# Expert layer of a two-block network: gates scattered into a DRAM table by accumulating indirect DMAs, first product expert by token, second product kept in PSUM

## Chip, core and metric

The kernel runs on one core of one Trainium2 chip. The metric is the device time of one execution in microseconds (us), and less is better.

## What is computed

The program runs two blocks of a network on 256 tokens of width 2048: a gated MLP and a stick-breaking attention, then a convolution and mLSTM mixer, and at the end a product-key expert layer with a layernorm before and after it. Only the expert layer is changed. Its reference, cut:

```python
q = (xt @ wq).reshape(-1, PEER_HEADS, 2, PEER_HALF)
s = jnp.einsum('thpc,hpnc->thpn', q, keys)
sv, si = lax.top_k(s, PEER_TOPK)
cand = (sv[:, :, 0, :, None] + sv[:, :, 1, None, :]).reshape(-1, PEER_HEADS, PEER_TOPK * PEER_TOPK)
cid = (si[:, :, 0, :, None] * N_KEYS + si[:, :, 1, None, :]).reshape(-1, PEER_HEADS, PEER_TOPK * PEER_TOPK)
top_s, top_j = lax.top_k(cand, PEER_TOPK)
eid = jnp.take_along_axis(cid, top_j, axis=-1)
gate = jax.nn.softmax(top_s.astype(jnp.float32), axis=-1)
act = jax.nn.gelu(jnp.einsum('thkd,td->thk', jnp.take(u, eid, axis=0), xt).astype(jnp.float32), approximate=False)
return jnp.einsum('thk,thkd->td', (gate * act).astype(xt.dtype), jnp.take(v, eid, axis=0))
```

There are 16384 experts (128 x 128 keys), 8 heads and 16 experts per head and token. Both kernels compute it densely: the product of all tokens with all of `u`, gelu, times a table of gates that is zero but for the chosen experts, times all of `v`.

## The kernel before

**Weights.** One list, `order`, names every weight tile (128 x 2048 floats, 1 MB) in the order of use. `Stream` loads them ahead on SP's queue (line 105) into 3 buffers `raw`. ScalarE copies each half tile to a float32r part `wh` (line 191, 6 buffers), VectorE makes the rest, `wl` (line 128, 5 buffers). A new tile is loaded when the second `wl` of the tile three before it is made.

**Products.** `gemm` computes a chunk, 256 tokens by 512 outputs, with three matmuls of 512 columns for each block of 128 inputs and each half of the tokens (lines 315 to 317); the activations are the stationary operand. Its result is two PSUM tiles `acc` (two buffers each). Every 12 matmuls (a half tile) it calls `bg.step()`.

**Background work.** `bg` holds generators. Each step advances every one of them by a piece, so their instructions are recorded between the matmuls of the products. No scheduler moves them later: each engine and each DMA queue runs them in this order.

**Expert layer.** Four chunks make the queries (`wq`). For each, `route` finds the top 16 of the product keys for two heads: 26 pieces, in a chain of four routes, the reduces of line 1129 last. Beside them the first product runs: `NU` = 32 units of 512 experts, four weight tiles each; ScalarE applies gelu and SP writes the result to the DRAM tensor `Ad` (line 1255). After the last route, `gates_all` transposes indices and gates (line 1166) and makes the table of gates: for each token two matmuls' worth of one-hot rows, built by POOL (lines 1183, 1184) and VectorE (line 1181), a matmul of 256 columns (line 1199), an addition (line 1204), and writes of 512 KB to the DRAM tensor `Gd` (line 1206). `load_v` then loads `Ad` and `Gd` of two units on SP's queue (lines 1215, 1218). `prep_v` multiplies them and transposes the product on PE (line 1236) to get experts on the partitions. The second product runs 16 passes of 4 chunks with `gemm`, and VectorE adds each chunk to the residual `h_res` (line 1287).

```python
    RAW, HI, LO = 3, 6, 5
...
        if j == 1:
            del self.raw[i]
            self._load()
```

Of the kernel before, what the change touches and what calls it, by code (L numbers as in the profile page):

```python
# [7 lines left out]
U32 = mybir.dt.uint32  # L8
# [19 lines left out]
for _n, _w in (("ident", 128), ("le", 128), ("trineg", 128), ("mneg3", 384), ("mbig3", 384),  # L28
               ("iota", 128), ("one", 1), ("negone", 1), ("eps", 1), ("leps", 1)):
    CO[_n] = (sum(w for _, w in CO.values()), _w)  # L30
# [56 lines left out]
class Stream:  # L87
    """Weight tiles in the order of use: loaded ahead, split by halves into two float32r parts."""
# [78 lines left out]
def _block(ctx, tc, A, out):  # L167
# [135 lines left out]
    def gemm(xh, xl, kmap, evac, need={}, by_token=False):  # L303
# [3 lines left out]
        acc = [pp.tile([P, 512], F32, name=nm("acc"), tag=f"acc{t}", bufs=2) for t in range(2)]  # L307
        last = len(kmap) - 1

        def mm(t, kk, wh, wl, k, first, fin):  # L310
# [4 lines left out]
            E.matmul(acc[t], a, wa, start=first, stop=False)  # L315
            E.matmul(acc[t], a, wb, start=False, stop=False)  # L316
            E.matmul(acc[t], b, wa, start=False, stop=fin)  # L317
# [31 lines left out]
        r = evac(acc)  # L349
# [25 lines left out]
    def rstd_of(dst, var, eps):  # L375
        """(var + eps) ** -0.5, a square root and a Newton step."""
# [35 lines left out]
    # ================ layer 0: gated MLP with spatial gating ================  # L412
# [196 lines left out]
    # ================ layer 1: stick-breaking attention ================  # L609
# [47 lines left out]
    def staged(gens, gap=2):  # L657
        """Chains run one stage apart, with `gap` steps of other work between the stages."""
# [75 lines left out]
    def affine_prep(c, d, gname, bname):  # L734
        """h_res*c+d in place, then transposed with gain and bias into two parts."""
# [48 lines left out]
    def residual_affine(gname, bname, alloc):  # L784
        """Gain and bias on the residual itself, in the token layout."""
# [24 lines left out]
    # ================ mLSTM and convolution mixer ================  # L810
# [275 lines left out]
    def route(n, q, before):  # L1086
        """Top 16 of the products of keys for two heads; q: [128 tok, 2, 512]."""
# [8 lines left out]
        for t in range(2):  # L1096
# [13 lines left out]
            for hh in range(2):  # L1110
# [34 lines left out]
    def gates_all():  # L1145
        yield from wait(rts[-1])
        ex = et(0, [16, 16])
        tva = tvs.rearrange("p t h k -> p (t h) k")
        V.tensor_tensor(ex, tva, tva[:, :, 0:1].to_broadcast([P, 16, 16]), op=ALU.subtract)
        act(ex, ex, AF.Exp)  # L1150
        yield
        yield
        es = et(1, [512])[:, 0:16]
        V.tensor_reduce(es, ex, axis=mybir.AxisListType.X, op=ALU.add)
        V.reciprocal(es, es)
        for t in range(2):
            V.tensor_tensor(gat[:, t, 2].rearrange("p (h k) -> p h k", h=8), ex[:, t * 8:(t + 1) * 8],
                            es[:, t * 8:(t + 1) * 8, None].to_broadcast([P, 8, 16]), op=ALU.mult)
        yield
        yield  # L1160
        f5 = ft(5, [4, T])
        i0, i1, gh, gl = (f5[:, j] for j in range(4))
        for s_ in range(3):
            p = ps()
            for t in range(2):
                E.transpose(p[:, t * P:(t + 1) * P], gat[:, t, s_], ident)
            if s_ < 2:
                V.tensor_copy((i0, i1)[s_], p[:, :T])
            else:
                act(gh.bitcast(F32R), p[:, :T], AF.Copy)  # L1170
                V.tensor_tensor(gl, p[:, :T], gh, op=ALU.subtract)
        yield
        yield

        def build(t0):
            """One-hot rows of two tokens: gates (two parts) by first key, ones by second key."""
            a = et(rot("oha", (0, 1, 4)), [2, 2, P], F32R)
            c = et(rot("ohb", (2, 3, 5)), [2, P], F32R)
            for j in range(2):
                t = t0 + j  # L1180
                V.tensor_scalar(a[:, j, 0], C("iota"), i0[:, t:t + 1], gh[:, t:t + 1],  # L1181
                                op0=ALU.is_equal, op1=ALU.mult)
                nc.gpsimd.tensor_scalar(c[:, j], C("iota"), i1[:, t:t + 1], None, op0=ALU.is_equal)  # L1183
                nc.gpsimd.tensor_scalar(a[:, j, 1], C("iota"), i0[:, t:t + 1], gl[:, t:t + 1],  # L1184
                                        op0=ALU.is_equal, op1=ALU.mult)
            return a, c

        ready = [build(0)]
        yield
        ready.append(build(2))  # L1190
        yield
        for b in range(T // 8):
            gsb = ft(rot("gsb", (3, 6)), [8, P])
            for hb in range(4):
                t0 = b * 8 + hb * 2
                a, c = ready.pop(0)
                p = ps().rearrange("p (t s i) -> p t s i", t=2, s=2)
                for j in range(2):
                    E.matmul(p[:, j], c[:, j], a[:, j], start=True, stop=True)  # L1199
                if t0 + 4 < T:  # L1200
                    ready.append(build(t0 + 4))
                d = gsb[:, hb * 2:hb * 2 + 2]
                act(d, p[:, :, 0], AF.Copy)
                V.tensor_tensor(d, p[:, :, 1], d, op=ALU.add)  # L1204
                yield
            nc.sync.dma_start(out=Gd[:, b * 8:(b + 1) * 8, :], in_=gsb)

    gall = bg.add(gates_all())
    vin, wts = {}, {}

    def load_v(u):
        if u >= NU:
            return
        a = ft(4 + u % 2, [2, 512])
        nc.sync.dma_start(out=a, in_=Ad[u])
        g = ft(2 + u % 2, [2, 4, P])
        for t in range(2):
            nc.sync.dma_start(out=g[:, t], in_=Gd[4 * u:4 * u + 4, t * P:(t + 1) * P, :].rearrange("j t i -> t j i"))
        vin[u] = (a, g.rearrange("p t j i -> p t (j i)"))

    def prep_v(pr_):
        w16 = tile("xs", [NKT, T], F32R, bufs=4)
        wts[pr_] = (w16[:, 0:8], w16[:, 8:16])
        for j in range(2):
            a, g = vin.pop(2 * pr_ + j)
            for t in range(2):
                V.tensor_tensor(a[:, t], a[:, t], g[:, t], op=ALU.mult)
            yield
            yield
            put = split_ps(wts[pr_][0], wts[pr_][1], 4 * j)  # L1230
            for pr in range(2):
                p = ps()
                for jj in range(2):
                    for t in range(2):
                        k = pr * 2 + jj
                        E.transpose(p[:, jj * T + t * P:jj * T + (t + 1) * P], a[:, t, k * P:(k + 1) * P], ident)  # L1236
                put(pr, p)
                yield
# [149 lines left out]
```

## Time and profile before

| | |
|---|---|
| median of 3 runs | 3409.7 us (3409.08 to 3410.12) |
| span of the profiled execution | 3406.2 us |
| the median over that span | 3.5 us |
| busy PE, VectorE, ScalarE, POOL | 97%, 61%, 44%, 14% of the span |
| moved by DMA | 668.58 MB, 196 GB/s |

The profiled execution's own time is shown only as its span, from the first to the last instruction. Busy shares are over the whole span; a stage is read from stretches of it. PE counts as busy while a matmul is in the array, with ends that are modelled, so the pace of PE is read from the starts of matmuls and not from its busy share.

### The profile page before, as it was taken

How to read it: one execution, taken by the hardware profiler on the slowest of the kernel's cores; microseconds unless marked ns; L12 is line 12 of the kernel's file. 1: busy time of each engine (PE TensorE's matmuls, PEld its weight loads, DVE VectorE, ACT ScalarE, POOL GpSimd, SP SyncE). 2: the span in 40 equal slices, each digit the busy share in tenths (PEclk: the TensorE clock that was granted, in tenths of full speed). 3: DMA queues.
4: the chain of work that ended last, by engine and by line, in shares of the span. 5: the costliest groups of instructions: out<-in, count | busy, mean ns of one | idle time of the engine just before them, and what ended most of it. 6: DMA issues, size and time to landing. Idle time of an engine off the chain costs nothing.

```text
span 3406.2 us, 39023 instructions
## 1 busy us (share of the span) xinstructions
PE 3317.5 (97%) x14722; PEld 2663.5 (78%) x14722; DVE 2067.0 (61%) x2966; ACT 1507.0 (44%) x1781; POOL 485.7 (14%) x522
## 2 busy tenths in 40 slices
PE   8999999999999999999999999888899999999998
PEld 6888888888888878888878887666678888888886
DVE  6565555565555566555579886555554666666666
ACT  5444444444444544444354444443344444444443
POOL 0000000000000000000000008999970000000001
PEclk9999999999999999999999999999999999999999
DMA  7565555545554445545555656555666666666664
GB/s 260 206 209 175 184 185 179 181 165 180 173 173 161 171 151 201 176 148 198 174 190 206 210 192 218 195 187 197 201 225 235 233 218 222 232 227 233 221 211 148
DMA packets 134348, 668.58 MB, mean 196 GB/s; under 512 B 12177, under 2 KB 45073, under 8 KB 62609
## 3 DMA queue, kind: packets, MB, share of 16 engines
q1 hardware_dynamic: 134160, 666.10, 56.7%
q8 instruction: 116, 1.90, 0.2%
q14 instruction: 72, 0.58, 0.0%
HBM read 630.40 MB, written 35.65 MB: 196 GB/s over the span
## 4 chain that ended last, share of the span: by engine, by line
PE 84%; POOL 14%; DVE 1%; ACT 0%; issue 0%; DMA 0%; SPq 0%; DVEq 0%; POOLq 0%
PE acc L315 27%; PE acc L316 26%; PE acc L317 26%; POOL e L1183 8%; POOL e L1184 6%; PE ms L1236 1%; PE ms L361 1%; PE ms L515 0%; DVE res L1272 0%; PE ms L1099 0%; PE ms L642 0%; PE ms L631 0%; DVE wl L128 0%; PE ms L751 0%; DMA raw<-in_aw_v_dram 0%
## 5 line engine op out<-in xcount | busy, mean ns | idle before, releaser
L128 DVE TENSOR_TENSOR wl<-raw,wh 128x1024 fp32r<-128x1024 f32 x1106 | 1343.9, 1221 | 669.4 <-PE acc L316 552.5
L191 ACT ACTIVATE wh<-raw 128x1024 fp32r<-128x1024 f32 x1106 | 1168.0, 1059 | 1198.5 <-PE acc L317 1136.3
L315 PE MATMUL acc<-wh,xs 128*128 128x512 f32 x4160 | 1662.0, 400 | 13.4 <-ACT wh L191 9.0
L316 PE MATMUL acc<-wl,xs 128*128 128x512 f32 x4160 | 1646.5, 396 | 0.5 <-DVE wl L128 0.5
L317 PE MATMUL acc<-wh,xs 128*128 128x512 f32 x4160 | 1645.9, 396 | 0.0
L315 PEld LDWEIGHTS acc<-wh,xs 128*128 128x128 f32 x4160 | 783.2, 188 | 194.2 <-ACT wh L191 9.0
L317 PEld LDWEIGHTS acc<-wh,xs 128*128 128x128 f32 x4160 | 782.6, 188 | 189.8 <-DVE xs L766 0.4
L316 PEld LDWEIGHTS acc<-wl,xs 128*128 128x128 f32 x4160 | 783.3, 188 | 178.0 <-DVE wl L128 1.0
L1183 POOL TENSOR_SCALAR e<-con,f 128x128 fp32r<-128x128 f32 x256 | 273.7, 1069 | 2053.7 <-ACT f L191 2053.7
L1184 POOL TENSOR_SCALAR e<-con,f 128x128 fp32r<-128x128 f32 x256 | 208.6, 815 | 0.0
L191 ACT ACTIVATE f<-ms 128x256 f32<-128x256 f32 (+3 forms) x153 | 62.7, 418 | 291.5 <-PE ms L1199 264.6
L1204 DVE TENSOR_TENSOR f<-ms,f 128x256 f32<-128x256 f32 x128 | 54.3, 424 | 198.1 <-ACT f L191 198.1
L1275 POOL TENSOR_TENSOR res<-res,xs 128x512 f32<-128x512 f32 x6 | 9.7, 1645 | 861.6 <-DVE res L1272 861.6
L1199 PE MATMUL ms<-e,e 128*128 128x256 f32 x256 | 82.7, 328 | 48.4 <-POOL e L1184 48.4
L1199 PEld LDWEIGHTS ms<-e,e 128*128 128x128 f32 x256 | 47.8, 187 | 92.9 <-POOL e L1184 86.5
L368 DVE TENSOR_TENSOR xs<-ms,xs 128x512 fp32r<-128x512 f32 x76 | 52.0, 690 | 110.1 <-ACT xs L191 110.1
L315 PE MATMUL acc<-wh,f 128*128 128x512 f32 x256 | 102.2, 399 | 0.0
L191 ACT ACTIVATE xs<-ms 128x512 fp32r<-128x512 f32 x76 | 44.8, 597 | 128.9 <-PE ms L1236 121.4
L316 PE MATMUL acc<-wl,f 128*128 128x512 f32 x256 | 101.2, 395 | 0.0
L317 PE MATMUL acc<-wh,f 128*128 128x512 f32 x256 | 101.2, 395 | 0.0
L1287 DVE TENSOR_TENSOR res<-res,acc 128x512 f32<-128x512 f32 x120 | 79.7, 683 | 35.1 <-PE acc L317 35.1
L1181 DVE TENSOR_SCALAR e<-con,f 128x128 fp32r<-128x128 f32 x256 | 83.4, 365 | 0.0
(213 smaller groups left out, 1355.5 us busy)
## 6 DMA issues: line engine op xcount, KB each, us to landing
raw<-in_pu_dram SPq DMA_DIRECT2D x128, 1024.0 KB, 4.9
raw<-in_pv_dram SPq DMA_DIRECT2D x128, 1024.0 KB, 4.8
raw<-in_bwi_dram SPq DMA_DIRECT2D x64, 1024.0 KB, 4.7
raw<-in_w_dram SPq DMA_DIRECT2D x56, 1024.0 KB, 4.7
raw<-in_aw_u_dram SPq DMA_DIRECT2D x32, 1024.0 KB, 4.7
raw<-in_aw_z_dram SPq DMA_DIRECT2D x32, 1024.0 KB, 4.8
raw<-in_awo_dram SPq DMA_DIRECT2D x32, 1024.0 KB, 4.7
raw<-in_aw_v_dram SPq DMA_DIRECT2D x31, 1024.0 KB, 4.8
```

What stands on the lines that cost most here:

```text
L128: self.nc.vector.tensor_tensor(l, raw[:, j * 1024:(j + 1) * 1024], self.hi[q].bitcast(F32), op=ALU.subtract)
L191: S.activation(out, in_, func, **kw)
L315: E.matmul(acc[t], a, wa, start=first, stop=False)
L316: E.matmul(acc[t], a, wb, start=False, stop=False)
L317: E.matmul(acc[t], b, wa, start=False, stop=fin)
L368: V.tensor_tensor(xl[:, k0 + 2 * pr:k0 + 2 * pr + 2, :], p.rearrange("p (k t) -> p k t", k=2), hv.bitcast(F32), op=ALU.subtract)
L1181: V.tensor_scalar(a[:, j, 0], C("iota"), i0[:, t:t + 1], gh[:, t:t + 1], op0=ALU.is_equal, op1=ALU.mult)
L1183: nc.gpsimd.tensor_scalar(c[:, j], C("iota"), i1[:, t:t + 1], None, op0=ALU.is_equal)
L1184: nc.gpsimd.tensor_scalar(a[:, j, 1], C("iota"), i0[:, t:t + 1], gl[:, t:t + 1], op0=ALU.is_equal, op1=ALU.mult)
L1199: E.matmul(p[:, j], c[:, j], a[:, j], start=True, stop=True)
L1204: V.tensor_tensor(d, p[:, :, 1], d, op=ALU.add)
L1287: V.tensor_tensor(d, d, acc[t], op=ALU.add)
```

## The change

`gates_all` goes, and with it all one-hot rows. There are two DRAM tables `Gd`, one for each 128 tokens, expert by token. They are cleared by 32 writes of 512 KB on SP's queue during the output projection of the mixer. `route` also computes the softmax of its two heads and the flat index of each gate, and at its end issues 64 indirect DMAs on POOL: each adds 128 single gates, one of each token, into the table. `gemm_t`, the first product, has the weights as the stationary operand and 256 tokens as columns, so that `Ad` holds experts on the partitions and the transposes of `prep_v` go. The second product keeps its 256 x 2048 sums in all eight PSUM banks over the 16 passes and adds them to `h_res` once.

```diff
+    def gemm_t(xh, xl, evac):
+        acc = [pp.tile([P, 512], F32, name=nm("acc"), tag=f"acc{b}", bufs=2) for b in range(2)]
+        for kp in range(NKT // 2):
+            if kp:
+                bg.step()
+            wh, wl = st.next()
+            for k in range(2):
+                kk = kp * 2 + k
+                for b in range(4):
+                    o = acc[b // 2][:, (b % 2) * T:(b % 2 + 1) * T]
+                    c = k * 512 + b * P
+                    E.matmul(o, wh[:, c:c + P], xh[:, kk], start=kk == 0 and b % 2 == 0, stop=False,
+                             skip_group_check=True)
+                    E.matmul(o, wh[:, c:c + P], xl[:, kk], start=False, stop=False, skip_group_check=True)
+                    E.matmul(o, wl[:, c:c + P], xh[:, kk], start=False, stop=kk == NKT - 1,
+                             skip_group_check=True)
+        evac(acc)
+        bg.step()
...
+    def clear_gates():
+        z = ft(5, [1024])
+        nc.gpsimd.memset(z, 0.0)
+        yield
+        for i in range(16):
+            for t in range(2):
+                nc.sync.dma_start(out=Gd[t][i * 1024:(i + 1) * 1024].rearrange("(p a) c -> p (a c)", p=P), in_=z)
+                yield
+                yield
...
-                    V.tensor_reduce(gat[:, t, s_, head * 16:(head + 1) * 16], oh, axis=mybir.AxisListType.X,
-                                    op=ALU.add)
+                    V.tensor_reduce(key[:, s_], oh, axis=mybir.AxisListType.X, op=ALU.add)
+                V.scalar_tensor_tensor(key[:, 0], key[:, 1], float(P), key[:, 0], op0=ALU.mult, op1=ALU.add)
+                V.tensor_scalar(idx[:, t, head * 16:(head + 1) * 16], key[:, 0], float(P), C("pidx"),
+                                op0=ALU.mult, op1=ALU.add)
                 yield
+            hs = slice(2 * n, 2 * n + 2)
+            ex, es = gat[:, t, hs], ws[:, 192:194]
+            V.tensor_tensor(ex, tvs[:, t, hs], tvs[:, t, hs, 0:1].to_broadcast([P, 2, 16]), op=ALU.subtract)
+            act(ex, ex, AF.Exp)
+            yield
+            V.tensor_reduce(es, ex, axis=mybir.AxisListType.X, op=ALU.add)
+            V.reciprocal(es, es)
+            V.tensor_tensor(ex, ex, es[:, :, None].to_broadcast([P, 2, 16]), op=ALU.mult)
+        for c in range(32):
+            for t in range(2):
+                at = 32 * n + c
+                nc.gpsimd.indirect_dma_start(
+                    out=Gd[t].rearrange("e c -> (e c)")[:, None],
+                    out_offset=bass.IndirectOffsetOnAxis(ap=idx[:, t, at:at + 1], axis=0),
+                    in_=gat[:, t, 2 * n + c // 16, c % 16:c % 16 + 1], in_offset=None, compute_op=ALU.add)
...
-    def gates_all():
...
-            for t in range(2):
-                V.tensor_tensor(a[:, t], a[:, t], g[:, t], op=ALU.mult)
+            V.tensor_tensor(a, a, g, op=ALU.mult)
             yield
             yield
...
+            act(wh[:, 4 * j:4 * j + 4], a, AF.Copy)
+            V.tensor_tensor(wl[:, 4 * j:4 * j + 4], a, wh[:, 4 * j:4 * j + 4].bitcast(F32), op=ALU.subtract)
+            yield
             load_v(2 * pr_ + 2 + j)
 
     def first_v():
-        yield from wait(gall)
+        yield from wait(rts[-1])
+        while not all(u in done_u for u in range(2)):
+            yield
         load_v(0)
         load_v(1)
...
+    ys = [[pp.tile([P, 512], F32, name=nm("y"), tag="ms", bufs=4) for t in range(2)] for n in range(2)]
+    ys += [[pp.tile([P, 512], F32, name=nm("y"), tag=f"acc{t}", bufs=2) for t in range(2)] for n in range(2)]
...
-            gemm(*wts[pr_], [0, 4], ev, {}, pr_ == NP_ - 1 and n == 3)
+            fin = pr_ == NP_ - 1
+            gemm(*wts[pr_], [0, 4], ev if fin else None, {}, fin and n == 3, ys[n], pr_ == 0, fin)
```

The change moves instructions on SP and POOL. SP's queue before, late in the first product, where the first loads of the table stand (`raw` is a weight tile, `Ad` the gelus, `Gd` the table):

```order
L105 DMA raw409_18583<-in_pu_dram 128x2048 [waits DMAHW4_49,DVE_49,Activation_49]
L1255 DMA Ad_11789<-f0_1216_18597 128x1024 [waits Activation_49]
L1206 DMA Gd_11788<-f6_1207_18492 128x1024 [waits DMAHW2_49]
L1215 DMA f4_1217_18602<-Ad_11789 128x1024 [waits DMAHW3_49,PE_49]
L1218 DMA f2_1218_18604<-Gd_11788 128x4x128
L1218 DMA f2_1218_18604<-Gd_11788 128x4x128 [waits DMAHW6_49,DMAHW5_49,DMAHW2_49]
L1215 DMA f5_1219_18607<-Ad_11789 128x1024 [waits Pool_49]
L1218 DMA f3_1220_18609<-Gd_11788 128x4x128 [waits DMAHW7_49]
L1218 DMA f3_1220_18609<-Gd_11788 128x4x128 [waits DMAHW0_49]
L105 DMA raw410_18634<-in_pu_dram 128x2048 [waits DMAHW1_49,DVE_49]
```

SP's queue of the change, where the same loads stand now (`Gd0` and `Gd1` are the two tables, `DMASW` the semaphores of POOL's DMAs):

```order
L105 DMA raw345_15908<-in_pu_dram 128x2048 [waits DMAHW6_49,DVE_49]
L1243 DMA Ad_11167<-f0_747_15934 128x1024 [waits Activation_49]
L1205 DMA f4_748_16005<-Ad_11167 128x1024 [waits DMASW4_49,DMASW3_49,DMASW5_49,DMASW2_49,DMASW6_49,DMASW1_49,DMASW7_49,DMASW0_49,DVE_49]
L1208 DMA f2_749_16007<-Gd0_11165 128x4x128 [waits PE_49]
L1208 DMA f2_749_16007<-Gd1_11166 128x4x128 [waits DMAHW5_49]
L1205 DMA f5_750_16010<-Ad_11167 128x1024
L1208 DMA f3_751_16012<-Gd0_11165 128x4x128 [waits DMAHW7_49]
L1208 DMA f3_751_16012<-Gd1_11166 128x4x128 [waits DMAHW0_49]
L105 DMA raw346_16049<-in_pu_dram 128x2048 [waits DMAHW1_49,DVE_49]
```

Before, they stood behind the gelus of the 27th of 32 units; now they stand behind those of the 11th, in the piece that ends the last route, and the first of them waits for all of POOL's DMAs. The tile of `raw346` is the second of the 13th unit.

POOL's queue before, the first one-hot builds of 512:

```order
L1183 TENSOR_SCALAR e_753_14565<-con_71,f_748_14516 128x128
L1184 TENSOR_SCALAR e_752_14564<-con_71,f_748_14516 128x128
L1183 TENSOR_SCALAR e_755_14589<-con_71,f_748_14516 128x128
L1184 TENSOR_SCALAR e_754_14588<-con_71,f_748_14516 128x128
L1183 TENSOR_SCALAR e_760_14623<-con_71,f_748_14516 128x128
```

POOL's queue of the change, from its first indirect DMA on (256 in all, 64 for each route, the two tables in turn):

```order
L1182 DMA Gd0_11165<-f4_610_11825 2097152x1 [waits DMAHW4_49,DMAHW6_49,DMAHW2_49,DMAHW7_49,DMAHW0_49,DVE_49]
L1182 DMA Gd1_11166<-f4_610_11825 2097152x1 [waits DMAHW5_49,DMAHW3_49,DMAHW7_49,DMAHW1_49,DVE_49]
L1182 DMA Gd0_11165<-f4_610_11825 2097152x1 [waits DMASW0_49]
L1182 DMA Gd1_11166<-f4_610_11825 2097152x1 [waits DMASW1_49]
L1182 DMA Gd0_11165<-f4_610_11825 2097152x1 [waits DMASW2_49]
L1182 DMA Gd1_11166<-f4_610_11825 2097152x1 [waits DMASW3_49]
```

POOL builds nothing now; each of its DMAs but the first two waits until the DMA two before it, the last one into the same table, has landed.

## Rows read from the trace of the kernel before

**Rows 1.** The page: span, busy time by engine, granted clock in 40 slices

```profile
span 3406.2 us, 39023 instructions
PE 3317.5 (97%) x14722; PEld 2663.5 (78%) x14722; DVE 2067.0 (61%) x2966; ACT 1507.0 (44%) x1781; POOL 485.7 (14%) x522
...
PEclk9999999999999999999999999999999999999999
```

**Rows 2.** Windows: stretch, its sum, busy PE PEld DVE ACT POOL, clock, DMA, GB/s

```profile
1710.00:1720.00 10.00, 8.68 (x29) 6.83 (x30) 6.42 (x10) 6.33 (x10) 0.00 (x0) 0.66 0.31 105
...
1800.00:1900.00 100.00, 100.00 (x451) 81.08 (x451) 89.15 (x220) 45.10 (x50) 0.00 (x0) 1.00 0.60 209
...
2200.00:2300.00 100.00, 89.10 (x380) 66.88 (x378) 57.37 (x108) 40.90 (x62) 100.00 (x109) 1.00 0.59 193
...
3000.00:3100.00 100.00, 100.00 (x447) 80.70 (x447) 61.78 (x68) 40.89 (x43) 0.00 (x0) 1.00 0.66 233
```

**Rows 3.** Timeline of PE, one period of the one-hot stage: start us, length

```profile
2299.93 0.28 PE L1199 MATMUL ms<-e,e 128*128 128x256 f32 x1
...
2303.63 0.28 PE L1199 MATMUL ms<-e,e 128*128 128x256 f32 x1
```

**Rows 4.** By source, lines 1199 and 1166 on PE: durations ns, first and last start

```profile
L1199 PE MATMUL ms<-e,e x256: 275/281/388, 2064.7 to 2530.0; 128*128 128x256 f32 x128
...
L1166 PE MATMUL ms<-con,f x6: 271/272/273, 2052.8 to 2053.4; 128*128 128x128 f32 x6
```

**Rows 5.** Timeline of PE in the second product, transposes between matmuls

```profile
2555.44 0.60 PE L1236 MATMUL ms<-con,f 128*128 128x128 f32 x4
...
2558.68 0.60 PE L1236 MATMUL ms<-con,f 128*128 128x128 f32 x4
```

**Rows 6.** Groups by line, PE and PEld: count, busy us, mean ns

```profile
L1236 PE MATMUL ms<-con,f 128*128 128x128 f32 x256 | 38.3, 272 | 0.0
...
L822 PEld LDWEIGHTS ms<-xs,wl 128*128 128x128 f32 x16 | 3.0, 188 | 0.0
```

**Rows 7.** Timeline of PE, the mLSTM gates: 48 matmuls of 256 columns, weights stationary

```profile
1282.65 0.40 PE L316 MATMUL acc<-wl,xs 128*128 128x512 f32 x1
...
1285.22 0.28 PE L821 MATMUL ms<-xs,wh 128*128 128x256 f32 x1
...
1290.87 0.40 PE L315 MATMUL acc<-wh,xs 128*128 128x512 f32 x1
```

**Rows 8.** Timeline of VectorE: the last reduce of the first and the last route

```profile
1819.57 0.42 DVE L1129 TENSOR_REDUCE f<-e 128x16 f32<-128x256 f32 x1
...
2041.07 0.42 DVE L1129 TENSOR_REDUCE f<-e 128x16 f32<-128x256 f32 x1
```

**Rows 9.** Groups by line, POOL

```profile
L1183 POOL TENSOR_SCALAR e<-con,f 128x128 fp32r<-128x128 f32 x256 | 273.7, 1069 | 2053.7 <-ACT f L191 2053.7
L1184 POOL TENSOR_SCALAR e<-con,f 128x128 fp32r<-128x128 f32 x256 | 208.6, 815 | 0.0
```

**Rows 10.** DMA issues: count, KB each, median us from issue to landing

```profile
raw<-in_pu_dram SPq DMA_DIRECT2D x128, 1024.0 KB, 4.9
...
Gd<-f SPq DMA_DIRECT2D x32, 512.0 KB, 6.7
f<-Gd SPq DMA_DIRECT2D x64, 256.0 KB, 6.3
...
out_dram<-res SPq DMA_DIRECT2D x8, 256.0 KB, 2.0
```

**Rows 11.** By source, line 1218 (loads of the table): time to landing

```profile
DMA to landing us min/median/max: 3.0/6.3/8.1
```

**Rows 12.** Waits of SP's queue: us in total, times, longest

```profile
SPq L105 <- DVE wl L128: 2890.1, 535, 13.2
```

**Rows 13.** Groups by line, ScalarE and VectorE

```profile
L191 ACT ACTIVATE wh<-raw 128x1024 fp32r<-128x1024 f32 x1106 | 1168.0, 1059 | 1198.5 <-PE acc L317 1136.3 <-issue 29.0 <-DMA raw<-in_aw_v_dram 12.3
...
L1119 DVE TENSOR_SCALAR f<-f 128x16 uint32<-128x16 uint32 x16 | 2.8, 174 | 0.5
```

More of the change, by code (lines that the diff above doesn't have):

```diff
@@ L28 @@
 for _n, _w in (("ident", 128), ("le", 128), ("trineg", 128), ("mneg3", 384), ("mbig3", 384),
-               ("iota", 128), ("one", 1), ("negone", 1), ("eps", 1), ("leps", 1)):
+               ("iota", 128), ("pidx", 1), ("one", 1), ("negone", 1), ("eps", 1), ("leps", 1)):
     CO[_n] = (sum(w for _, w in CO.values()), _w)
@@ L300, in _block, with gemm @@
     ident = C("ident")
-    def gemm(xh, xl, kmap, evac, need={}, by_token=False):
-        acc = [pp.tile([P, 512], F32, name=nm("acc"), tag=f"acc{t}", bufs=2) for t in range(2)]
+    def gemm(xh, xl, kmap, evac, need={}, by_token=False, acc=None, opens=True, closes=True):
+        if acc is None:
+            acc = [pp.tile([P, 512], F32, name=nm("acc"), tag=f"acc{t}", bufs=2) for t in range(2)]
         last = len(kmap) - 1
@@ L314, in mm @@
             wb = wl[:, k * 512:(k + 1) * 512]
-            E.matmul(acc[t], a, wa, start=first, stop=False)
+            E.matmul(acc[t], a, wa, start=first and opens, stop=False)
             E.matmul(acc[t], a, wb, start=False, stop=False)
-            E.matmul(acc[t], b, wa, start=False, stop=fin)
+            E.matmul(acc[t], b, wa, start=False, stop=fin and closes)
         for i, k0 in enumerate(kmap):
@@ L1042, in _block @@
     bg.finish(*[yt5[k] for k in (("o", 0), ("o", 1), ("cB", 0))])
+    Gd = [dr.tile([NE, P], F32, name=f"Gd{t}") for t in range(2)]
+    Ad = dr.tile([NU, P, 4, T], F32, name="Ad")
+    def clear_gates():
[7 more added lines that the diff above has]
+                yield
+    clear = bg.add(clear_gates())
     for n in range(4):
@@ L1066, in _block @@
     nc.sync.dma_start(out=keysT, in_=A["keysT"])
-    Gd = dr.tile([P, T, P], F32, name="Gd")
-    Ad = dr.tile([NU, P, 2, 512], F32, name="Ad")
     f4 = ft(4, [1024])
-    gat = f4[:, :768].rearrange("p (t s c) -> p t s c", t=2, s=3)
-    tvs = f4[:, 768:].rearrange("p (t h k) -> p t h k", t=2, h=8)
+    idx = f4[:, 0:256].bitcast(U32).rearrange("p (t c) -> p t c", t=2)
+    gat = f4[:, 256:512].rearrange("p (t h k) -> p t h k", t=2, h=8)
+    tvs = f4[:, 512:768].rearrange("p (t h k) -> p t h k", t=2, h=8)
     def topk16(vals, mx, ix):
@@ L1143, in _block @@
         gemm(x3h, x3l, FULL, ev, prep3 if n == 0 else {})
-    def gates_all():
[L1146 to L1155, printed above, removed]
-        for t in range(2):
[L1157 to L1206, printed above, removed]
@@ L1208, in _block @@
-    gall = bg.add(gates_all())
     vin, wts = {}, {}
@@ L1223, in prep_v @@
         wts[pr_] = (w16[:, 0:8], w16[:, 8:16])
+        wh, wl = wts[pr_]
         for j in range(2):
             a, g = vin.pop(2 * pr_ + j)
-            for t in range(2):
-                V.tensor_tensor(a[:, t], a[:, t], g[:, t], op=ALU.mult)
+            V.tensor_tensor(a, a, g, op=ALU.mult)
             yield
             yield
[L1230 to L1238, printed above, removed]
+            act(wh[:, 4 * j:4 * j + 4], a, AF.Copy)
+            V.tensor_tensor(wl[:, 4 * j:4 * j + 4], a, wh[:, 4 * j:4 * j + 4].bitcast(F32), op=ALU.subtract)
+            yield
             load_v(2 * pr_ + 2 + j)
     def first_v():
-        yield from wait(gall)
+        yield from wait(rts[-1])
+        while not all(u in done_u for u in range(2)):
+            yield
         load_v(0)
@@ L1247, in first_v @@
         yield from prep_v(0)
+    done_u = set()
     fv = bg.add(first_v())
@@ L1252, in ev @@
             a = ft(rot("act", (0, 1)), [2, 512])
-            for t in range(2):
-                act(a[:, t], acc[t], AF.Gelu)
-            nc.sync.dma_start(out=Ad[u], in_=a)
-        gemm(x3h, x3l, FULL, ev)
-    bg.finish(gall, fv)
+            for b in range(2):
+                act(a[:, b], acc[b], AF.Gelu)
+            nc.sync.dma_start(out=Ad[u], in_=a.rearrange("p b (e t) -> p (b e) t", e=2))
+            done_u.add(u)
+        gemm_t(x3h, x3l, ev)
+    bg.finish(fv)
     bg.drain()
```

28 lines of the change are left out of this document (13 added, 15 removed).

## The prediction

> **What bounds the kernel now.** I read the page first. PE is busy for 97% of the span, no other engine for more than 61%, and the granted clock is at its upper level, 2.4 GHz, in every slice [rows 1]. So a change is worth what it takes off PE's queue, or adds to it as waits. The windows say where PE does not run full: in 2200 to 2300 us it is at 89 us of 100 while POOL is at 100; in 1800 to 1900 VectorE is at 89, and PE is full all the same [rows 2]. The first is the one-hot stage. Its pace is read from starts: from one pair of one-hot matmuls to the next lie 3.70 us, and in them 12 matmuls of the first product and the pair [rows 3].
>
> **The unit of PE's work.** From 1282.65 to 1285.22 us lie 11 matmuls of 512 columns: 233.6 ns each. From 1285.22 to 1290.87 lie 48 of 256 columns with weights stationary, three to a block, as the new first product has them: 117.7 ns each, or 235.4 for two [rows 7]. Their weight loads last 188 ns and overlap [rows 6].
>
> **Part 1, the one-hot table goes.** 128 pairs run from 2064.7 to 2530.0 us [rows 4], 127 periods in 465.3 us. Their other work is 127 x 12 x 0.2336 = 356.0 us. What is left, and goes, is 109 us. The six transposes of line 1166 end with it, under 1 us.
>
> **Part 2, the transposes of the second product go.** Four transposes and 12 matmuls take 2558.68 - 2555.44 = 3.24 us [rows 5]; less 12 x 0.2336 = 2.80 that is 0.44 us. There are 256 / 4 = 64 such groups [rows 6]: 28 us.
>
> **Part 3, the first product by token.** 32 units x 4 tiles x 24 = 3072 matmuls of 512 columns become 6144 of 256. At 235.4 - 233.6 = 1.8 ns a pair that adds 6 us.
>
> **Part 4, sums kept in PSUM.** 120 additions leave VectorE; PE did not wait for them, so this is worth nothing. The banks of chunks 0 and 1 were idle, those of 2 and 3 are needed two chunks after the last unit's gelu. The first chunk's end in the last pass has the same VectorE work as before.
>
> **Part 5, clearing.** 32 writes of 512 KB replace 32 writes of the same size later [rows 10]. 18 of them stand in a row on SP's queue ahead of the fifth query tile: 9.4 MB. A tile of 1 MB lands in 4.9 us, of which a small transfer takes 2.0 as well, so 2.9 us for each MB [rows 10] and 27 us in all. PE has four query tiles in hand, 4 x 24 x 0.2336 = 22 us, and the pause of the layernorm ahead of them. I take 0; without that cover it costs 15 us at most.
>
> **Part 6, the routes get longer.** Each has 28 pieces for 26. Small VectorE work grows by some 32 x 2 operations of 0.17 us [rows 13] and 8 softmaxes of about 1 us: 20 us over four routes of 75 us, in a stretch where VectorE is at 89% [rows 2]. The five `wl` buffers hide it; I take 0, and 10 us if they don't.
>
> So far: -109 - 1 - 28 + 6 = **-132 us**, if nothing new waits.
>
> **Part 7, the scatter, and who waits for it.** This decides the sign. The first route's last reduce is at 1819.6 us and the fourth's at 2041.1 [rows 8]. With two more pieces of 2.80 us for each route so far, and some 2 us of part 3, the first 64 DMAs are ready at about 1826 us and the last 64 at 2066. Only two of them are in flight at once, because each waits for the one two before. With r the time per DMA, half of one DMA's time from issue to the next start on its table, the last lands at T = the later of 1826 + 256 r and 2066 + 64 r (the two routes between never set it by much).
>
> No row shows a DMA from POOL. The nearest to its issue are POOL's one-hot builds, 1.07 and 0.82 us, mean 0.94 [rows 9]. The nearest to its landing, from below, is the write of 256 KB to DRAM at the program's end, with no weights beside it, 2.0 us [rows 10]; the shortest load of the table amid the weights took 3.0 us [rows 11]; from above the write of 512 KB to the table, 6.7 us [rows 10]. A scatter moves 512 bytes, but beside weights, in a stretch where the DMA engines are 60% busy [rows 2]. I take 2.65 us, between the quiet write and the fastest load: r = (0.94 + 2.65) / 2 = 1.8 us. Ends: 2.0 / 2 = 1.0 us, if the issue lies inside the landing, and (1.07 + 6.7) / 2 = 3.9 us. Nothing excludes either.
>
> Who waits: the first load of `Ad`, on SP's queue, in the piece after the last route. Behind it on the same queue stand five more loads and then every weight tile from the second of the 13th unit on. SP runs its queue in order, and it is kept just ahead of PE: its waits for `wl` buffers are 2890 us in 535 times [rows 12]. PE reaches the 12th unit's start at 2066 us: 2052.8, line 1166, which stood four pieces behind the last route [rows 4], and 4 x 2.80 for the eight more pieces of the routes less those four, and some 2 of part 3. It then holds five tiles, those of that unit and the first of the next, 5 x 48 x 0.1177 = 28 us, and stops at 2094. After T, 2 MB of loads go first (2 x 2.9 us), then the tile lands (4.9, rows 10) and its first half is copied (1.06, rows 13): 12 us. When PE resumes after the pause of the layernorm, the granted clock of the next 10 us is 0.66 [rows 2], so some 7 us are at its lower level, 1.2 GHz, and 3 are lost; the same is put here. So PE loses S = T + 15 - 2094 = T - 2079.
>
> With r = 1.8: T = 1826 + 461 = 2287, S = 208 us. **Sum: -132 + 208 = +76 us**, made on the span of 3406.2 us; the median lies 3.5 us above it, and I carry that over: 3409.7 + 76 = **3486 us**. The sign changes at S = 132, T = 2211, r = 1.50 us, a DMA of 3.0 us.
>
> The Trainium skill, "DMA: Bandwidth & Descriptors", section "Anatomy of one DMA — SWDGE (gpsimd) path", puts a DMA issued from POOL at about 2.0 us fixed plus bytes over 436 GB/s; by it r would be 1.0 and the time 3329 us, against 3486 by the rows; that is the lower end of rival B. No run here shows it yet.
>
> **Rivals.**
> - **B, the scatter is quick enough (faster).** The wait stays, but DMAs take under 3.0 us. For it: the quiet write's 2.0 us, and that each moves 512 bytes. Against: that write had no weights beside it, and has no indices to read. With r = 1.4: T = 2184, S = 105, 3383 us. With r = 1.0, the last route's own 64 set the end: T = 2130, S = 51, 3329 us. It decides at r = 1.50.
> - **C, the scatter is much slower (far slower).** Loads of the table take 6.3 us in the middle [rows 10], and 128 single elements may fare like their 512 short packets. With r = 2.8: T = 2543, S = 464, 3742 us. At r = 3.9 it is 4023 us.
> - **D, the wait hides.** T before 2079 gives the whole -132: 3278 us. Against it: the last 64 DMAs alone need 64 us from 2066 on at r = 1.0.
> - **E, the new first product does not run at the pace of the mLSTM gates.** If each of its 6144 matmuls waited for its whole load of 188 ns, it would add 3072 x (376 - 234) ns = 436 us: about 3920 us with the forecast's wait. Rows 7 speak against it: 48 ran at 117.7 ns.
>
> **How the numbers follow.** The forecast, A, r from 1.53 to 2.4 us (its own range 3416 to 3639): 0.47. C: 0.15. E: 0.01. B: 0.31, of which the lower end, r of 1.2 or less, 0.11. D: 0.01. Within 0.2% (7 us, about what a measurement of this kernel can tell from no change; r from 1.48 to 1.53): 0.05. So faster 0.32, same 0.05, slower 0.63. The range goes from B's lower end, 3329, to C, 3742: below and above it stay about 0.04 and 0.10, and the small bounds of parts 5 and 6 lie inside.
>
> **What would show it.** Right: VectorE, SP and PE idle together from about 2094 us on for some 200 us, the wait of SP named as POOL's scatter; POOL issues 256 DMAs at some 1.8 us each from about 1826 us; no idle PE in the old one-hot stage; matmuls of 256 columns at 118 ns in the first product; the second product without transposes, 28 us shorter. Wrong: if the stop of PE is below 132 us, the kernel is faster and the size of r failed; if there is none, the step that SP's wait starves PE failed; if PE is slower in the first product outside the stop, part 3 failed; if PE waits around 1740 us, part 5 did.

## The result, and the profile after

The kernel after takes 3594.4 us (median of 4 runs, 3592.56 to 3596.41), the kernel before 3409.85 beside it: a ratio of 1.0543 [1.0528, 1.0558], so 185 us slower. The forecast was 76 us slower, 3486. The profiled execution took 3595.13 us, with a span of 3593.3, against the 3406.2 of [rows 1].

The page of the kernel after: span, PE's busy time, and in 40 slices PE's busy tenths and its granted clock:

```profile
span 3593.3 us, 42805 instructions
PE 3239.0 (90%) x17276; PEld 2757.0 (77%) x17276; DVE 1883.8 (52%) x2454; ACT 1481.8 (41%) x1638; POOL 438.1 (12%) x267
...
PE   8999999999999999999999930019999999999998
...
PEclk9999999999999999999999975559999999999999
```

PE was busy for 97% of the span before [rows 1]; now there is one hole, about three and a half slices of 90 us, and the granted clock falls to its lower level (0.5, 1.2 GHz) in it. The windows of the same stretches as in [rows 2], busy PE, PEld, DVE, ACT, POOL, then clock, DMA share and GB/s:

```profile
2000.00:2100.00 100.00, 100.00 (x851) 99.88 (x849) 72.67 (x179) 42.99 (x46) 68.51 (x37) 1.00 0.57 159
2200.00:2300.00 100.00, 0.00 (x0) 0.00 (x0) 0.00 (x0) 0.00 (x0) 83.44 (x55) 0.50 0.22 0
3000.00:3100.00 100.00, 100.00 (x431) 80.12 (x430) 54.91 (x47) 43.74 (x42) 0.00 (x0) 1.00 0.67 237
```

From 2200 to 2300 us only POOL works, and no byte of weights moves. Before, that stretch was the one-hot stage, with PE at 89 us. Of the 851 matmuls from 2000 to 2100 us 843 are the first product's, of 256 columns, and 8 a route's; the starts from 2093.80 to 2099.80 us lie 117.6 ns apart, as in [rows 7]. The group of PE with all the idle time of the hole (left of the bar busy us and mean ns, right of it the idle time and what ended it), the wait of SP's queue (total, times, longest), and SP's timeline around it:

```profile
L368 PE MATMUL acc<-xs,wh 128*128 128x256 f32 x2048 | 573.1, 280 | 310.4 <-ACT wh L191 310.4
```

```profile
SPq L1205 <- DMA Gd<-f: 322.4, 4, 316.9
```

```profile
2074.86 0.33 SPq L1243 DMA_DIRECT2D Ad<-f  x1
2397.83 0.33 SPq L1205 DMA_DIRECT2D f<-Ad  x1
2398.21 0.98 SPq L1208 DMA_DIRECT2D f<-Gd  x2
...
2400.86 1.85 SPq L105 DMA_DIRECT2D raw<-in_pu_dram  x3
```

The first load of `Ad` waits for the last scatter until 2397.8 us, the weights behind it with it, and PE, 310 us idle, waits for a weight tile (`wh`). The place and the chain are the forecast's; the scatter's pace is not. The indirect DMAs by source (duration of the issue, the time that it holds POOL; POOL's idle time that ended with a landing, us and times; the time from the issue's start to the landing), and two windows of them alone (busy POOL with the number issued, clock, DMA share, GB/s):

```profile
L1182 POOL DMA_INDIRECT Gd<-f x256: 1543/1545/2589, 1792.7 to 2394.7; - x128
...
  DMA Gd<-f: 71.3, 43
...
DMA to landing us min/median/max: 2.9/3.0/8.8
```

```profile
1832.00:2080.00 248.00, 162.07 (x87) 1.00 0.69 207
2104.00:2390.00 286.00, 237.18 (x154) 0.50 0.22 0
```

Beside the kernel's other work 87 DMAs take 248 us, **2.85 us each**; in the stop 154 take 286 us, **1.85 us each**. So the pace before the stop, not the one in it, was far from the forecast's 1.8, and the slow part has two candidates. Around 2088 us, where PE is about to run dry, the trace parts them. POOL's timeline:

```profile
2080.51 2.54 POOL L1182 DMA_INDIRECT Gd<-f  x1 [0.31 <-issue]
2083.35 2.51 POOL L1182 DMA_INDIRECT Gd<-f  x1 [0.30 <-issue]
2086.16 2.52 POOL L1182 DMA_INDIRECT Gd<-f  x1 [0.30 <-issue]
2088.99 1.55 POOL L1182 DMA_INDIRECT Gd<-f  x1 [0.30 <-issue]
```

and VectorE's:

```profile
2083.22 1.22 DVE L128 TENSOR_TENSOR wl<-raw,wh 128x1024 fp32r<-128x1024 f32 x1 [1.59 <-PE acc L371]
2086.04 1.23 DVE L128 TENSOR_TENSOR wl<-raw,wh 128x1024 fp32r<-128x1024 f32 x1 [1.60 <-PE acc L371]
```

PE runs until 2100, yet the issue falls from 2.52 to 1.55 us as soon as VectorE's last `wl` is made. So one candidate is VectorE (the issue stretches), the other the weights' traffic (the landing stretches, POOL waits for it).

### The profile page after: what moved, and what is told of

The parts are those of the page before. It is cut to its first block, busy times and chain, and to the rows that moved or that the text cites. A ratio compares the mean times of both kernels' runs of the same rounds, so it can differ in the third digit from the quotient of the medians.

```text
span 3593.3 us, 42805 instructions
## 1 busy us (share of the span) xinstructions
PE 3239.0 (90%) x17276; PEld 2757.0 (77%) x17276; DVE 1883.8 (52%) x2454; ACT 1481.8 (41%) x1638; POOL 438.1 (12%) x267
## 3 DMA queue, kind: packets, MB, share of 16 engines
q8 instruction: 135, 2.21, 0.2%
## 4 chain that ended last, share of the span: by engine, by line
PE 86%; POOL 7%; DMA 2%; issue 2%; DVE 1%; ACT 1%; SPq 0%; DVEq 0%; ACTq 0%
PE acc L317 15%; PE acc L318 15%; PE acc L319 15%; POOL Gd L1182 7%; PE y L317 7%; PE y L319 7%; PE y L318 7%; PE acc L370 6%; PE acc L368 6%; PE acc L371 6%; DMA Gd<-f 2%; PE ms L384 1%; PE ms L538 0%; DMA raw<-in_wq_dram 0%; DVE wl L128 0%
## 5 line engine op out<-in xcount | busy, mean ns | idle before, releaser
L317 PE MATMUL acc<-wh,xs 128*128 128x512 f32 x2112 | 848.2, 402 | 15.5 <-ACT wh L191 9.0
L368 PE MATMUL acc<-xs,wh 128*128 128x256 f32 x2048 | 573.1, 280 | 310.4 <-ACT wh L191 310.4
L318 PE MATMUL acc<-wl,xs 128*128 128x512 f32 x2112 | 838.2, 397 | 0.5 <-DVE wl L128 0.5
L319 PE MATMUL acc<-wh,xs 128*128 128x512 f32 x2112 | 838.1, 397 | 0.0
L368 PEld LDWEIGHTS acc<-xs,wh 128*128 128x128 f32 x2048 | 385.8, 188 | 310.6 <-ACT wh L191 310.6
L370 PE MATMUL acc<-xs,wh 128*128 128x256 f32 x2048 | 574.1, 280 | 0.0
L371 PE MATMUL acc<-xs,wl 128*128 128x256 f32 x2048 | 572.3, 279 | 0.5 <-DVE wl L128 0.5
L317 PEld LDWEIGHTS acc<-wh,xs 128*128 128x128 f32 x2112 | 399.1, 189 | 112.7 <-ACT wh L191 9.0
L1182 POOL DMA_INDIRECT Gd<-f x256 | 427.3, 1669 | 413.1 <-DVE f L1178 273.9
L319 PEld LDWEIGHTS acc<-wh,xs 128*128 128x128 f32 x2112 | 398.7, 189 | 97.1 <-DVE xs L789 0.9
L318 PEld LDWEIGHTS acc<-wl,xs 128*128 128x128 f32 x2112 | 399.3, 189 | 93.8 <-DVE wl L128 1.0
L317 PE MATMUL y<-wh,xs 128*128 128x512 f32 x1024 | 403.5, 394 | 0.0
L319 PE MATMUL y<-wh,xs 128*128 128x512 f32 x1024 | 403.5, 394 | 0.0
L318 PE MATMUL y<-wl,xs 128*128 128x512 f32 x1024 | 403.5, 394 | 0.0
L370 PEld LDWEIGHTS acc<-xs,wh 128*128 128x128 f32 x2048 | 385.3, 188 | 0.0
L1218 DVE TENSOR_TENSOR f<-f,f 128x1024 f32<-128x1024 f32 x32 | 39.0, 1218 | 316.6 <-DMA f<-Gd 316.6
```

The costliest lines, as they stand in the source:

```text
L317: E.matmul(acc[t], a, wa, start=first and opens, stop=False)
L319: E.matmul(acc[t], b, wa, start=False, stop=fin and closes)
L368: E.matmul(o, wh[:, c:c + P], xh[:, kk], start=kk == 0 and b % 2 == 0, stop=False, skip_group_check=True)
L370: E.matmul(o, wh[:, c:c + P], xl[:, kk], start=False, stop=False, skip_group_check=True)
L371: E.matmul(o, wl[:, c:c + P], xh[:, kk], start=False, stop=kk == NKT - 1, skip_group_check=True)
L1182: nc.gpsimd.indirect_dma_start(out=Gd[t].rearrange("e c -> (e c)")[:, None], out_offset=bass.IndirectOffsetOnAxis(ap=idx[:, t, at:at + 1], ...
```

## The experiments

The theory: parts 1 to 6 gave what the sum says, and the loss is SP's in-order wait for the scatter; the scatter is slow beside weights and VectorE work. Rivals: the new products themselves are slower, or the scatter hurts in another way than by the stop.

### Taking the wait away, or the scatter

**e3_none**: `for c in range(32)` at the scatter becomes `range(0)`; all gates are left out and the table stays zero.

> The changed kernel without any indirect DMA (all gates are left out; the tables are zero). Theory: no stop of PE in the first product, and the time is that of the other parts of the change alone, 3410 - 132 + 5 = 3283 us. Rival (part of the loss lies in other parts, such as the longer routes or the product by token): above 3300 us.

3281.3 us, 0.9619 [0.9603, 0.9635]. The group that sat idle for 310 us:

```profile
L368 PE MATMUL acc<-xs,wh 128*128 128x256 f32 x2048 | 572.2, 279 | 0.0
```

The second product takes 716 us for its 3072 matmuls, 2546.6 to 3262.7: 233 ns each, with nothing between them. Without the scatter the change saves 126 us of span and 130 of the median, so the whole loss comes with the scatter. That it is the wait, and not the DMAs as such, is for the next run to show.

**e1_late**: the loads are recorded behind the 30th unit of the first product.

```diff
-        while not all(u in done_u for u in range(2)):
+        while not all(u in done_u for u in range(30)):
```

> The changed kernel with one number altered: the first loads of the table are issued after 30 units of the first product instead of 2. Theory (PE's 310 us of idle come from SP's queue standing behind the scatter, and from nothing else): the stop goes whole, 3594 - 310 = about 3285 us, and the scatter, no longer helped by an idle chip, ends between 2420 and 2490 us. Rival (the scatter itself slows the weights or the engines, wherever its loads stand): PE still idles 100 us or more between 1830 and 2500 us, above 3385 us.

3313.7 us, 0.9717 [0.9701, 0.9733]: one constant turns 185 us lost into 97 won. But it was 29 us short of the forecast. All four routes now scatter beside weights, the last DMA is issued at 2543.2 us and SP waits again:

```profile
SPq L1205 <- DMA Gd<-f: 46.0, 4, 40.5
```

```profile
2080.00:2500.00 420.00, 286.86 (x148) 1.00 0.72 209
```

148 DMAs in 420 us: 2.84 us each, as in the loaded part of the kernel after. PE idles 32 us. A wait moved 425 us later (SP's write of `Ad` ahead of it stands at 2499.8 instead of 2074.9) is still a wait when what it waits for slows down with it.

**e2_half**: `range(16)` at the scatter, half the DMAs; the other half of the gates is left out.

> The changed kernel with 32 instead of 64 indirect DMAs for each route (the gates of one of its two heads are left out); the loads stand where the change has them. Theory (the stop is as long as the scatter's rest): 32 DMAs fit beside the next route, the last 32 start at about 2073 us and end near 2145, PE idles some 60 us, 3345 us. Rival (the stop is a fixed cost of the first loads or of the wait itself): PE idles about 310 us as before, 3594 us.

3364.4 us (one run), the last DMA issued at 2162.1, PE idle 77.8 us. The stop follows the scatter's end. It was 18 us longer than expected: the 32 DMAs of a route did not all fit beside the next route, so the last route's first one left at 2103.6 and not at 2073.

**e8_last**: as e1_late, with all 32 units ahead (`range(NU)`).

> The changed kernel with the first loads of the table issued after all 32 units, so that no weight tile stands behind the wait. Theory (the scatter, at 2.75 us a DMA beside weights, ends near 2550 us whatever is done with the loads, and what is left to pay is the load, product and split ahead of the second product): PE idles 12 to 20 us there, about 3297 us. Rival (the loads want their place two units ahead, or else their own chain of load, product and split lies open): 3314 us or more.

3307.8 us, 0.9707 [0.9691, 0.9723]. In the profiled run, the fastest of four (3303.5 us), the scatter ends at 2556 and PE idles 20.8 us at the second product's start. The first product no longer stops, but the scatter is as long as before. The median is 11 us worse than expected, and hardly apart from e1_late (0.9717 [0.9701, 0.9733]).

**e7_early**: e1_late, and 12 DMAs of the first 128 tokens are issued as soon as their half of the first route is done (lines of `route` reordered).

> The kernel of the late loads (after 30 units), with 12 DMAs of the first 128 tokens issued as soon as these have their gates, in place of in turn with those of the other tokens; the number of DMAs is the same. Theory (a scatter of 711 us beside a first product of 720 us is too long by some 30 us, and POOL stands idle for 37 us behind its first DMA): the scatter ends near 2513 instead of 2546 us, PE does not stop, 3314 - 30 = 3284 us. Rival (the end of the scatter is set by the last route, or the stop is of the loads themselves): 3305 us or more.

A miss: 3324.0 us, 0.9748 [0.9732, 0.9764], no better than e1_late. The 12 DMAs, all on one table, took 64 us, 1790.3 to 1854.3: 5.3 each, one landing after the other. One chain instead of two gave back most of the earlier start: by 1853 us 12 had left, against 10 in e1_late. The rest then went at 2.88 us each against 2.81; why is not shown.

### What sets the scatter's pace

**e5_dve**: in the stop VectorE gets 60 two-input products of 512 columns (SBUF), 60 one-input scalings of 1024 (SBUF) and 60 copies of 512 from PSUM; ScalarE gets 60 copies.

```diff
...
+        for _ in range(60):
+            V.tensor_tensor(d[:, 0:512], d[:, 512:1024], m, op=ALU.mult)
+        for _ in range(60):
+            V.tensor_scalar(d, d, 1.0, None, op0=ALU.mult)
+        for _ in range(60):
+            V.tensor_copy(d[:, 0:512], p)
+        for _ in range(60):
+            act(d, d, AF.Copy)
```

> The changed kernel, with work that computes nothing added to the stop of PE, where no weights move: 60 VectorE products of two SBUF inputs (512 columns each), then 60 VectorE scalings of one SBUF input (1024), then 60 VectorE copies out of PSUM (512), then 60 ScalarE copies (1024). A quiet indirect DMA takes POOL 1.54 us. Theory (VectorE's work on SBUF holds up the issue on POOL): issue lengthens to 2.5 us or more under the two-input products, and is 1.54 us under ScalarE's copies; landings are not waited for. Rival (only DMA traffic lengthens the scatter): 1.54 us under all four.

3672.9 us (one run; the dummy work is in it). POOL beside the products, the scalings and the PSUM copies:

```profile
2101.55 1.88 POOL L1182 DMA_INDIRECT Gd<-f  x1 [0.30 <-issue]
...
2150.39 1.88 POOL L1182 DMA_INDIRECT Gd<-f  x1 [0.30 <-issue]
...
2189.77 1.55 POOL L1182 DMA_INDIRECT Gd<-f  x1 [0.30 <-issue]
```

The DMAs alone, in the stretch of the products, the scalings, the PSUM copies, and after them:

```profile
2100.00:2130.00 30.00, 25.74 (x15) 0.56 0.19 0
2130.00:2180.00 50.00, 42.71 (x23) 0.50 0.20 0
2184.00:2220.00 36.00, 30.00 (x20) 0.50 0.24 0
2230.00:2400.00 170.00, 140.91 (x92) 0.50 0.23 0
```

The issue is 1.88 us beside either SBUF work and 1.55 beside PSUM copies or none. The effect is there, without any traffic or PE, but smaller than expected: these operations last 0.69 us each, the kernel's `wl` 1.22. From issue to issue lie 2.18 us, three of these operations with the 0.03 between them. ScalarE's copies ran only after the scatter, so ScalarE's part stays untested.

**e6_dma**: 90 loads of 512 KB are put in the stop, with VectorE idle.

```diff
+        for k in range(90):
+            nc.sync.dma_start(out=ft((2, 3, 5)[k % 3], [1024]), in_=A["pv"][k // 4 % NU, k % 4][:, 0:1024])
```

> The changed kernel, with 90 loads of 512 KB that nothing reads ahead of the first loads of the table on SP's queue, so that they run in the stop of PE while VectorE is idle. Theory (weight traffic lengthens the landing, and with two in flight POOL then waits for it; the issue itself does not change): issue stays at 1.54 us, waits of POOL for a landing appear, and a DMA takes 2.2 to 2.8 us in place of 1.85 while the loads run. Rival (VectorE alone slows the scatter): 1.85 us throughout.

3671.4 us (one run; the loads are in it). POOL's timeline amid the loads:

```profile
2104.08 1.54 POOL L1182 DMA_INDIRECT Gd<-f  x1 [3.56 <-DMA Gd<-f]
2105.93 1.54 POOL L1182 DMA_INDIRECT Gd<-f  x1 [0.30 <-issue]
2111.38 1.54 POOL L1182 DMA_INDIRECT Gd<-f  x1 [3.90 <-DMA Gd<-f]
```

and the DMAs amid the loads and after them:

```profile
2100.00:2240.00 140.00, 58.62 (x39) 0.50 0.90 286
2250.00:2450.00 200.00, 166.19 (x108) 0.50 0.24 0
```

Traffic leaves the issue at 1.54 us and puts the time into the wait for the landing of the DMA two before: 3.6 us a DMA at 286 GB/s, more than expected, and 1.85 without. The two causes are separate: VectorE stretches the issue, traffic the landing.

**e4_four**: as the kernel after, with four tables in turn, so four DMAs in flight (the added pair is not cleared, nor read by the second product).

```diff
+    Gx = [dr.tile([NE, P], F32, name=f"Gx{t}") for t in range(2)]
...
-                    out=Gd[t].rearrange("e c -> (e c)")[:, None],
+                    out=(Gd, Gx)[c % 2][t].rearrange("e c -> (e c)")[:, None],
```

> The changed kernel with four tables in turn instead of two (every second gate goes to a table that nothing reads and nothing clears), so that four indirect DMAs may be in flight. Theory (POOL's own issue, 1.54 us and 0.30 between, sets the pace, and landings only add the 71 us of waits seen): the scatter ends near 2327 us, PE idles 240 us, 3524 us. Rival (the landing of 3 us with two in flight sets the pace): it ends before 2150 us, PE idles under 65 us, under 3350 us.

3559.2 us (one run), PE idle 272.9 us: 37 us less stop, and 33 more than the theory's 240. The waits for a landing are gone (1.5 us in all), and what they cost beside the weights is won; in the stop the issue sets the pace in any case.

**e9_four_late**: four tables and the loads behind 30 units.

> The kernel of four tables in turn (every second gate goes where nothing reads it), with the loads after 30 units. Theory (beside weights the landing, with two in flight, holds POOL back by some 0.7 us a DMA; the issue, stretched by VectorE, takes the rest): with four in flight the waits for a landing go nearly all, a DMA takes 2.0 to 2.2 us, the scatter ends between 2345 and 2400 us, PE does not stop, 3284 us. Rival (the issue is the limit beside weights too): 2.7 us a DMA, the scatter ends near 2545 us, 3314 us.

3283.2 us (one run) and no stop, since the scatter's last issue came at 2491.5, ahead of the loads; in e1_late it came at 2543.2. Most of these 52 us were won beside the routes, where VectorE does their small operations too. The same 100 us in e1_late and here:

```profile
1950.00:2050.00 100.00, 66.83 (x34) 1.00 0.71 212
```

```profile
1950.00:2050.00 100.00, 86.90 (x43) 1.00 0.74 202
```

Behind the routes the pace missed the expected 2.0 to 2.2 us and was the rival's 2.7: the waits for landing were gone (1.2 us in all) and the issue took their place. POOL:

```profile
2200.36 2.52 POOL L1183 DMA_INDIRECT Gx<-f  x1 [0.30 <-issue]
2203.19 2.52 POOL L1183 DMA_INDIRECT Gd<-f  x1 [0.30 <-issue]
```

and VectorE:

```profile
2200.24 1.23 DVE L128 TENSOR_TENSOR wl<-raw,wh 128x1024 fp32r<-128x1024 f32 x1 [1.60 <-PE acc L371]
2203.07 1.23 DVE L128 TENSOR_TENSOR wl<-raw,wh 128x1024 fp32r<-128x1024 f32 x1 [1.60 <-PE acc L371]
```

One issue begins 0.12 us into each `wl` and the next stands behind it: 2.52 + 0.30 = 2.82 us, which is a half tile of the first product, 24 x 0.1177. POOL is locked to VectorE's rhythm.

How it comes to be locked can be read in e8_last, where landings shift the starts of the issues. POOL:

```profile
2119.96 1.54 POOL L1182 DMA_INDIRECT Gd<-f  x1 [1.93 <-DMA Gd<-f]
2121.80 1.88 POOL L1182 DMA_INDIRECT Gd<-f  x1 [0.30 <-issue]
2124.84 1.67 POOL L1182 DMA_INDIRECT Gd<-f  x1 [1.16 <-DMA Gd<-f]
2126.81 2.52 POOL L1182 DMA_INDIRECT Gd<-f  x1 [0.30 <-issue]
```

and VectorE:

```profile
2118.21 1.22 DVE L128 TENSOR_TENSOR wl<-raw,wh 128x1024 fp32r<-128x1024 f32 x1 [1.60 <-PE acc L371]
2121.04 1.23 DVE L128 TENSOR_TENSOR wl<-raw,wh 128x1024 fp32r<-128x1024 f32 x1 [1.60 <-PE acc L371]
2123.86 1.23 DVE L128 TENSOR_TENSOR wl<-raw,wh 128x1024 fp32r<-128x1024 f32 x1 [1.60 <-PE acc L371]
2126.69 1.23 DVE L128 TENSOR_TENSOR wl<-raw,wh 128x1024 fp32r<-128x1024 f32 x1 [1.60 <-PE acc L371]
```

An issue that begins while a `wl` runs ends 1.42 us after that `wl`: 0.25 us of it are left at 2124.84, and the issue takes 1.67; 1.11 are left at 2126.81, and it takes 2.52. An issue that begins between two `wl` takes 1.54, even where the next `wl` starts under it (2119.96). All 71 issues from 2110 to 2310 us keep to this within 0.02 us. So the issue waits for the VectorE operation that it finds running. With nothing else to wait for, the next issue then begins 1.42 + 0.30 us after that `wl`, when the next one, 1.60 us after it, is already running: that is the lock.

**e10_four_split and e11_last_split** cut the `wl` operation into two of 512 columns, e10 on e9_four_late and e11 on e8_last.

```diff
-        self.nc.vector.tensor_tensor(l, raw[:, j * 1024:(j + 1) * 1024], self.hi[q].bitcast(F32),
-                                     op=ALU.subtract)
+        for s in (slice(0, 512), slice(512, 1024)):
+            self.nc.vector.tensor_tensor(l[:, s], raw[:, j * 1024 + s.start:j * 1024 + s.stop],
+                                         self.hi[q].bitcast(F32)[:, s], op=ALU.subtract)
```

> The kernel of four tables and late loads, with each of VectorE's subtractions for the weights (line 128, 1024 columns, 1.23 us) cut into two of 512 columns, all through the program. Theory (an indirect DMA's issue on POOL is held until the VectorE operation then running ends: 2.52 us with one of 1.23 us in it, one DMA for each half tile of 2.82 us): an operation of half the length holds it for half as long, issue falls to 1.9 to 2.2 us, and the scatter ends before 2440 instead of near 2491 us; the time stays at 3283 us, since nothing waited for it there. Rival (the issue is long for the weights' traffic or for PE, not for VectorE): issue stays at 2.52 us and the scatter ends near 2490 us.

> The kernel with the loads after 32 units and two tables, with the same cut of VectorE's subtractions. Theory: with two in flight the landing beside weights (4.8 us in the middle) takes over as the limit, so that the pace gains less, 2.5 to 2.7 us a DMA; the scatter ends 20 to 60 us earlier than 2553 us, before the first product does, and PE idles some 12 us for load, product and split: 3295 us. Rival (the scatter's pace does not hang on VectorE): 3308 us as without the cut.

e10: 3283.2 us (one run), the last DMA issued at 2324.2. e11: 3310.2 us, 0.9705 [0.9688, 0.9721], no gain over e8_last's 3307.8, against the 3295 expected. (Its profiled run, with the last issue at 2569.8, was its slowest, 3319.0 us.) The same 200 us of scatter, beside the same weights, in four kernels: e8_last (two tables, `wl` whole), e9_four_late (four, whole), e11_last_split (two, cut) and e10_four_split (four, cut):

```profile
2110.00:2310.00 200.00, 139.34 (x71) 1.00 0.72 213
```

```profile
2110.00:2310.00 200.00, 178.05 (x73) 1.00 0.73 209
```

```profile
2110.00:2310.00 200.00, 118.06 (x69) 1.00 0.70 208
```

```profile
2110.00:2310.00 200.00, 166.09 (x106) 1.00 0.80 209
```

In us per DMA:

| | `wl` whole | `wl` cut |
|---|---|---|
| two tables, two in flight | 2.82 | 2.90 |
| four tables, four in flight | 2.74 | 1.89 |

**Two limits of almost the same size stand one behind the other.** With two in flight POOL waits for a landing, for 50 of the 200 us in e8_last and for 67 in e11_last_split, where the landings (median 4.9 and 5.2 us in the stretch) leave 2.82 and 2.90 us a DMA. With four in flight and `wl` whole it waits for none, and the locked issue allows one in 2.82 us (67 of its 73 issues there last 2.51 to 2.54). In this stretch taking either away alone brings next to nothing; both together bring the pace of the quiet stretch, 1.89 against 1.85. With `wl` cut, an issue waits only for the half that it finds running, and takes 1.54 to 1.74 us in e10_four_split. By what an issue is held, and why PSUM copies do not hold it, is not shown.

## Why the prediction was wrong

The direction, the place and the chain held; **the step that failed is the size of r in part 7**, and in it that one r was taken for both stretches. That the time still lies in the forecast's own range, 3416 to 3639 us, is luck: r came to 2.21, inside its 1.53 to 2.4, only as the mean of two paces that it did not foresee.

- **Part 7, r.** The text took (0.94 + 2.65) / 2 = 1.8 us. Measured from the second DMA (1832.1; the first, for the other 128 tokens, left at 1792.7 already) to the last landing (2397.8) it is 565.7 / 256 = 2.21 us, a mean of 2.85 beside weights and 1.85 in the stop. The issue is 1.54 + 0.30 us where the one-hot builds of [rows 9] had lent 0.94; it lasts up to 2.52 beside `wl`. The landing is 3.0 us in the quiet and 4.8 to 5.4 at the median beside weights (e8_last, e9_four_late), against 2.65. Beside weights the 87 DMAs took 87 us more than at 1.85 each: about 28 in longer issues, about 58 in waits for a landing. That the quiet r came out at 1.85 is a coincidence: there POOL does not wait for a landing, so the formula's half of a chain doesn't apply, and the issue alone sets it.
- **T.** 2397.8 against 2287, 111 us: 6 from the start (1832 for 1826), 256 x 0.41 = 105 from r. This is the whole miss: 3594.4 - 3486 = 108.
- **The stop.** PE stopped at 2100 (forecast 2094) and resumed at 2410.5, 13 us after T (forecast 12). S = T - 2079 with the measured T gives 319; PE idled 310 and lost a few more at the lower clock.
- **Parts 1 to 4 and 6.** -132 with nothing waiting. e3_none gives -126 to -130 with part 5's cost in it: right as a sum; no run takes the parts apart. Matmuls of 256 columns come at 117.6 ns (rival E gone), and there are no transposes.
- **Part 5** was probably not quite hidden (no run leaves the clearing out): from 1710 to 1750 us PE is busy 34.6 us for 38.1 before, with 365 GB/s against 171, and the first route's key scores on PE start 5 us later (1751.5 for 1746.3). Inside its bound of 15.
- **Rivals.** C was nearer than the forecast's own r while weights moved, 2.85 against its 2.8; but once PE had stopped, the traffic that slowed the scatter stopped too, which kept the time far from C's 3742. B needed DMAs below 3.0 us throughout; only the quiet ones come to 3.0. D's time is what e9_four_late and e10_four_split reach, by later loads and not by D's T before 2079.
- **The page's rule.** The Trainium skill's 2.0 us fixed ("DMA: Bandwidth & Descriptors", "Anatomy of one DMA — SWDGE (gpsimd) path") does not fit this accumulating indirect DMA: its shortest landing, with 512 bytes, was 2.9 us, and r never came near 1.0.

The best version of this work that computes everything is e8_last, 3307.8 us: 101 us faster than the kernel before beside it (3408.4), 287 faster than the change as made. What the four tables would bring beyond it, up to some 25 us by e9_four_late, was not tried in full: they would have to be cleared, loaded and added, twice the table's traffic.

## What to carry to other kernels

Before a wait is put on an in-order queue, ask what stands behind it; here it was the weights, and moving the wait behind the last unit was worth 287 us. A price read from another operation on the same engine is no price: where nothing like the new operation is in the trace, give it two paces, one beside the kernel's traffic and one without. When taking away one of two suspected limits changes little, take both away before dropping either, and ask in which stretch it was taken away: four tables alone paid beside the routes and not behind them.

## What the runs showed of the hardware

- An accumulating indirect DMA of 128 single floats holds POOL for 1.54 us and 0.30 more to the next; it lands in 3.0 us with no other traffic.
- Its issue waits for the VectorE operation in SBUF that runs when it begins, and ends 1.42 us after it (e8_last, `wl`): up to 2.52 us beside two-input operations of 1.22 us, 1.88 beside operations of 0.69 us in a row, 1.55 beside PSUM copies of 0.69 us. An operation that starts under it does not stretch it.
- Its landing depends on traffic: 4.8 to 5.4 us at the median beside 210 GB/s, up to 9.6; beside 286 GB/s, with VectorE idle, two in flight took 3.6 us each.
- While PE stood still the granted clock was 0.50. In the first 10 us of the work that followed (2411 to 2421) it was 0.80, and 1.00 behind that, so the hole cost little beyond its length.
